# Attention scores: K's low part times Q's high part alone, on halves of the array's rows

## The chip, the core and the metric

The kernel runs on one core of a Trainium2 chip. The metric is device time in microseconds (us) of one execution. TensorE (PE) multiplies matrices in a 128 x 128 array: it loads a stationary operand (LDWEIGHTS), streams the moving operand's columns past it and writes to PSUM. VectorE (DVE), ScalarE (ACT) and GpSimd (POOL) work element by element, SyncE (SP) starts most DMAs. Each engine runs its own instructions in order and waits on semaphores for the others.

## What is computed

Two layers of a hybrid encoder on 1280 tokens (1024 of a prompt, 256 of a sample). The change lies in layer 0's attention. It has 8 heads of a dilated sliding-window mixture (branch a, three patterns) and 8 query heads of grouped-query attention over 2 K/V heads (branch b), all of 64 channels:

```python
s = jnp.einsum('bqhgd,bkhd->bhgqk', qblk, k, preferred_element_type=jnp.float32) * (Dh ** -0.5)
p = jax.nn.softmax(s, axis=-1)
return jnp.einsum('bhgqk,bkhd->bqhgd', p, vf)          # branch b
...
s = jnp.where(valid, s, -jnp.inf)                        # branch a, for each pattern
lse = jax.nn.logsumexp(s, axis=-1); p = jnp.exp(s - lse[..., None])
```

## The kernel before

Everything is f32. For the large products an operand is split in two: hi, which is the value rounded to the matmul's type (fp32r), and lo, the rest. PE then adds up hi·hi, hi·lo and lo·hi (`token_mm`).

Tokens stand in ten tiles of 128 (tiles 0 to 7 the prompt, 8 and 9 the sample). `start` projects x to q, k, v; its step `kvb` (L448) also makes branch b's K. `attention0` then runs 80 items: 4 head pairs of branch b with ten tiles each, then 4 of branch a (units 1 to 4). An item is 128 queries of two heads. For a prompt tile the keys are 8 blocks of 128 in b and 6 in a (these 64 items are called long); for a sample tile 2.

K of a head pair (KH, KL): `k_split` (L334) writes hi and lo of K, each channel twice, to `kd`; `k_trans` (L341) transposes them with 4 PE transposes into PSUM (M in the attention, tr in `start`), and ACT (KH, L349) and DVE (KL, L350) copy them out, scaled. Both halves of the 128 rows hold the same 64 channels. Branch a makes the next unit's K while it works on the present one (`nstep`); branch b makes unit 1's, a tile every fourth item. b's K comes from `start`.

One item i, in the source's order:
- `q_split`: POOL writes Q's hi and lo side by side; `q_trans` (L557): two PE transposes to M, DVE copies them to QS (L563). Rows 0 to 63 of QS are Q's hi, rows 64 to 127 its lo.
- `scores` (L566), a head at a time: QS times KH, then QS times KL, in parts of 512 or 256 columns, on all 128 rows (L587). So all four products of hi and lo are taken. Then DVE's minimum (b: L604; a: with the mask, L598) and ACT's exp (L605, L602). S has two PSUM buffers of 1024 columns.
- `trans` (L608), of item i-1: PE transposes P block by block to T (two PSUM buffers of 512 columns, L615), ACT (L619) and for the last chunk DVE (L617) copies them out.
- `pv` (L627), of item i-2: a transpose of the reciprocal row sums to M (L638, copied by ACT), then V times P on the array's column halves, a head on each (`tile_position`, L645), then DVE's scaling and a DMA.

M and O have one PSUM buffer each. Among the items stand steps of `ada` (modulation vectors for layer 1, matmuls on column strips, L225, every fourth item of b) and of `w_out` (splitting the next weights, ACT and POOL or DVE, every fourth item of a). The source's order isn't the engines' order: a list scheduler in the framework places the instructions by costs and priorities of its own.

Of the kernel before, what the change touches and what calls it, by code (L numbers as in the profile page):

```python
# [18 lines left out]
P = 128  # L19
# [30 lines left out]
class Trunk:  # L50
# [280 lines left out]
        nc.gpsimd.tensor_add(a[:, :n], a[:, :n], b[:, :n])  # L331
        return a

    def k_split(self, kd, k):  # L334

        src = k.rearrange("p (h d) -> p h d", d=HD).unsqueeze(2).to_broadcast([P, 2, 2, HD])
        self.nc.gpsimd.tensor_copy(kd[:, :, 0].bitcast(F32R), src)
        self.nc.gpsimd.tensor_sub(kd[:, :, 1], src, kd[:, :, 0])
        return kd

    def k_trans(self, kd, ps, K, t):  # L341

        nc = self.nc
        ps = ps.rearrange("p (b n) -> p b n", n=P)
# [10 lines left out]
    def start(self):  # L355
# [4 lines left out]
        with ExitStack() as s:  # L360
# [95 lines left out]
            def kvb(t, z):  # L456
                z = z[0]
                r = norm(z[:, :P], 2)
                a = self.rope(z[:, :P], tabs["cosBk"], tabs["sinBk"], 2, 16, t)
                scaled(a, r, 2)  # L460
                kds[t] = self.k_split(t2p.tile([P, 2, 2, 2, HD], F32, name="kd", bufs=3), a[:, :P])
# [36 lines left out]
    def attention0(self):  # L498
        nc, I, tc = self.nc, self.I, self.tc
        self.oT = [self.dram.tile([P, KB, P], F32, name=f"oT{t}") for t in range(NT)]  # L500
        with ExitStack() as s:
# [22 lines left out]
            def k_unit(u):  # L524

                cols = slice(u * P, (u + 1) * P)
                K = self.k_tiles(kp) if u % 2 == 0 else self.k_tiles(self.kbp)

                def load(t):
                    kt = ap.tile([P, P], F32, name="kt", bufs=3)  # L530
                    nc.sync.dma_start(kt, self.zd["ka"][:, t, cols])
                    return kt

                def step(t, kt):
                    self.k_trans(self.k_split(ap.tile([P, 2, 2, 2, HD], F32, name="kd"), kt), self.ps("M"), K, t)
# [13 lines left out]
                it["q"] = q  # L549

            def q_split(it):
                qs = ap.tile([P, 2, 2, HD], F32R, name="qs")
                src = it["q"].rearrange("p (h d) -> p h d", d=HD)
                nc.gpsimd.tensor_copy(qs[:, :, 0], src)
                it["split"] = nc.gpsimd.tensor_sub(qs[:, :, 1], src, self.f(qs[:, :, 0]))
                it["qs"] = qs

            def q_trans(it):
                ps = self.ps("M")
                for h in range(2):  # L560
                    nc.tensor.transpose(ps[:, h * P:(h + 1) * P], self.f(it["qs"][:, h]).rearrange("p a d -> p (a d)"), self.ident)
# [4 lines left out]
            def scores(it, h):  # L566

                br, t = it["br"], it["t"]
                K, kh = it["K"], it["kh"][h]
                blk = lambda X: X[:, kh].rearrange("p (b n) -> p b n", n=P)  # L570
# [8 lines left out]
                S = pb(self.ps("S"))  # L579
                outs, n = [], 0  # L580
                for p in parts:
                    m = len(range(*p.indices(12)))
                    outs.append((S[:, n:n + m], p))
                    n += m
# [3 lines left out]
                pe = ap.tile([P, 8, P], F32, name="pe", bufs=3)  # L588
                st = ap.tile([P, 4], F32, name="st", bufs=8)
                if br == "a":  # L590
                    if t < 8:
                        masks_ = [mask1[:, 3 - cq:7 - cq], pb(mask2[:, hq, cq])]
                    else:
                        masks_ = [pb(masks[:, t - 8])]
                    init, c = NEG, 0
                    for (o, p), mk in zip(outs, masks_):
                        m = o.shape[1]
                        nc.vector.tensor_tensor_reduce(pe[:, c:c + m], o, mk, 1.0, init, op0=OP.add, op1=OP.min,  # L598
                                                       accum_out=st[:, c // 4:c // 4 + 1])
                        init = st[:, c // 4:c // 4 + 1]  # L600
                        c += m
                    it["exp"] = nc.scalar.activation(pe[:, :n], pe[:, :n], AF.Exp, bias=init, scale=-1.0, accum_out=st[:, 2:3])  # L602
                else:
                    nc.vector.tensor_reduce(st[:, 0:1], S[:, :n].rearrange("p b n -> p (b n)"), axis=AX.X, op=OP.min)  # L604
                    nc.scalar.activation(pe[:, :n], S[:, :n], AF.Exp, bias=st[:, 0:1], scale=-1.0, accum_out=st[:, 2:3])  # L605
                it["pe", h], it["sum", h], it["n"] = pe, st[:, 2:3], n

            def trans(it, h):  # L608
                n = it["n"]
# [17 lines left out]
            def pv(it):  # L627
# [12 lines left out]
                nc.scalar.activation(rs, r[:, :P], AF.Copy)  # L640
                o = self.ps("O")
                for b in range(n):
                    for h in range(2):
                        kh = it["kh"][h]
# [20 lines left out]
            for i in range(N + 2):  # L665
# [1139 lines left out]
```

## Time and profile before

| | us |
|---|---|
| median of 3 runs | 3232.96 (3232.84 to 3234.95) |
| the profiled execution | 3234.79 |
| its span, first to last instruction | 3233.0 |
| attention stage, 366.3 to 804.9 | 438.6 |
| branch b, 366.3 to 604.2 | 237.9 |
| branch a, 604.2 to 804.9 | 200.7 |

The mean granted clock was 0.989 of full speed. In the rows below, MATMUL rows are PE's; a timeline row merges successive instructions of one kind and runs from the first's start to the last's modelled end. `128*64` is an instruction on 128 rows and 64 columns of the array, `64*128` one on 64 rows. "Idle" counts only time in which no modelled duration runs. A row of stretches (rows 2) holds: the stretch, its length; the busy time (and count) of PE, PEld, DVE, ACT, POOL; the granted clock, the DMA share, GB/s. A wait (rows 3) holds: us in total, times, longest. A group (rows 4, 7) holds: line, engine, operation, out<-in, shapes, count | busy us, mean ns | idle before it and what ended that.

### The profile page before, as it was taken

The page shows a single profiled execution, that of the slowest core. Times are in us where ns is not written, and L with a number is a line of the kernel's source. Part 1 is how long each engine was busy: PE and PEld are TensorE (multiplying, and loading weights), DVE is VectorE, ACT ScalarE, POOL GpSimd, SP SyncE. Part 2 cuts the span into 40 slices and gives each one's busy share as a digit, 9 for nine tenths or more (in the row PEclk, how much of TensorE's full clock was granted, in tenths as well). Part 3 has the DMA queues.
Part 4 walks back from the last instruction along what each step waited for, and adds up shares of the span by engine and source line. Part 5 has one row for each costly group of instructions (what it writes and reads, how often), then busy time and mean ns, then how long its engine had stood idle before and what let it go on. Part 6 is the DMA issues. An engine that isn't in the chain of part 4 may idle for free. (4 is left out here: it accounts for less than half of the span.)

```text
span 3233.0 us, 49122 instructions
## 1 busy us (share of the span) xinstructions
PE 3125.5 (97%) x18045; PEld 2588.7 (80%) x18045; DVE 1870.6 (58%) x3339; ACT 1435.7 (44%) x2921; POOL 815.3 (25%) x844
## 2 busy tenths in 40 slices
PE   7999999999999999999997998999899999999998
PEld 4777788888788888888886897889677888888886
DVE  4632356677677777544586025137678767644556
ACT  4411366677444444443465225124454444443344
POOL 2421122353014554400000211202214555500000
PEclk9999999999999999999998999999999999999999
DMA  8546622122635666755575313212643666675576
GB/s 268 168 139 212 195 70 74 47 71 57 204 100 176 220 225 214 271 170 177 171 236 171 110 56 101 63 35 66 182 153 113 230 223 219 231 235 172 175 231 207
DMA packets 312790, 520.43 MB, mean 161 GB/s; under 512 B 43093, under 2 KB 172293, under 8 KB 312421
## 3 DMA queue, kind: packets, MB, share of 16 engines
q1 hardware_dynamic: 312405, 516.89, 49.3%
q8 instruction: 142, 2.33, 0.3%
q14 instruction: 99, 0.81, 0.1%
q0 software_dynamic: 144, 0.39, 0.0%
HBM read 359.71 MB, written 157.48 MB: 160 GB/s over the span
## 5 line engine op out<-in xcount | busy, mean ns | idle before, releaser
L1112 PE MATMUL d<-w1l,sh 128*128 128x512 f32 x1120 | 438.2, 391 | 4.6 <-DVE w1l L94 4.6
L1111 PE MATMUL d<-w1h,sh 128*128 128x512 f32 x1120 | 435.9, 391 | 3.6 <-ACT sh L93 2.9
L1113 PE MATMUL d<-w1h,sl 128*128 128x512 f32 x1120 | 437.3, 392 | 1.4 <-DVE ss L99 1.1
L94 DVE TENSOR_TENSOR w1l<-raw,w1h 128x512 fp32r<-128x512 f32 x440 | 356.1, 818 | 115.7 <-ACT w1h L93 112.8
L94 DVE TENSOR_TENSOR sl<-sraw,sh 128x640 fp32r<-128x640 f32 (+2 forms) x256 | 194.7, 762 | 309.6 <-ACT sh L93 309.1
L850 PE MATMUL u<-hTh,w1l 128*128 128x512 f32 (+1 forms) x1056 | 359.2, 340 | 9.4 <-DVE w1l L94 9.4
L850 PE MATMUL u<-hTh,w1h 128*128 128x512 f32 (+1 forms) x1056 | 360.0, 341 | 2.0 <-ACT H L1004 1.7
L850 PE MATMUL u<-hTl,w1h 128*128 128x512 f32 (+1 forms) x1056 | 359.9, 341 | 0.1
L93 ACT ACTIVATE sh<-sraw 128x640 fp32r<-128x640 f32 (+2 forms) x256 | 172.7, 675 | 393.3 <-PE d L1112 367.2
L93 ACT ACTIVATE w1h<-raw 128x512 fp32r<-128x512 f32 x444 | 275.2, 624 | 141.1 <-PE u L850 112.1
L283 PE MATMUL z<-wh,hTh 128*128 128x512 f32 (+2 forms) x800 | 275.3, 362 | 2.9 <-ACT wh L93 1.7
L285 PE MATMUL z<-wh,hTl 128*128 128x512 f32 (+2 forms) x800 | 269.9, 354 | 1.7 <-DVE hTl L165 1.7
L283 PE MATMUL z<-wl,hTh 128*128 128x512 f32 (+2 forms) x800 | 270.0, 354 | 1.1 <-DVE wl L94 0.5
L1112 PEld LDWEIGHTS d<-w1l,sh 128*128 128x128 f32 x1120 | 210.7, 188 | 51.2 <-DVE w1l L94 8.0
L1111 PEld LDWEIGHTS d<-w1h,sh 128*128 128x128 f32 x1120 | 210.9, 188 | 50.5 <-ACT sh L93 5.5
L1113 PEld LDWEIGHTS d<-w1h,sl 128*128 128x128 f32 x1120 | 210.7, 188 | 48.2 <-DVE sl L94 5.4
L850 PEld LDWEIGHTS u<-hTh,w1l 128*128 128x128 f32 x1056 | 202.8, 192 | 31.4 <-DVE w1l L94 9.8
L850 PEld LDWEIGHTS u<-hTh,w1h 128*128 128x128 f32 x1056 | 202.9, 192 | 24.7 <-ACT H L1004 1.9
L850 PEld LDWEIGHTS u<-hTl,w1h 128*128 128x128 f32 x1056 | 203.0, 192 | 22.3 <-DVE hTl L165 1.1
L283 PEld LDWEIGHTS z<-wh,hTh 128*128 128x128 f32 x800 | 146.0, 189 | 37.4 <-issue 9.1
L285 PEld LDWEIGHTS z<-wh,hTl 128*128 128x128 f32 x800 | 146.2, 189 | 26.4 <-DVE hTl L165 3.5
L283 PEld LDWEIGHTS z<-wl,hTh 128*128 128x128 f32 x800 | 146.5, 189 | 19.6 <-DVE wl L94 1.9
(371 smaller groups left out, 6412.3 us busy)
## 6 DMA issues: line engine op xcount, KB each, us to landing
raw<-in_w_ff SPq DMA_DIRECT2D x128, 512.0 KB, 4.2
sraw<-hd SPq DMA_DIRECT2D x192, 320.0 KB, 3.0
wada<-in_w_ada SPq DMA_DIRECT2D x44, 1024.0 KB, 5.4
hd<-H SPq DMA_DIRECT2D x64, 640.0 KB, 4.0
wd<-raw SPq DMA_DIRECT2D x64, 512.0 KB, 3.0
raw<-in_w_ff SPq DMA_DIRECT2D x128, 256.0 KB, 3.7
raw<-wd SPq DMA_DIRECT2D x128, 256.0 KB, 3.2
hd<-part SPq DMA_DIRECT2D x96, 320.0 KB, 3.4
```

The source lines that it names most:

```text
L93: self.nc.scalar.activation(hi, src, AF.Copy)
L94: (eng or self.nc.vector).tensor_sub(lo, src, self.f(hi))
L283: nc.tensor.matmul(o, hi[:, k, sl], w[k][i][:, c], start=first and i == 0, stop=False)
L285: nc.tensor.matmul(o, lo[:, k, sl], w[k][0][:, c], start=False, stop=last)
L850: self.nc.tensor.matmul(o, a[:, k], b, start=(start and k == 0 and i == 0), stop=(stop and k == 3 and i == 2))
L1111: nc.tensor.matmul(ps, o[0][:, sl], w[0], start=first, stop=False)
L1112: nc.tensor.matmul(ps, o[0][:, sl], w[1], start=False, stop=False)
L1113: nc.tensor.matmul(ps, o[1][:, sl], w[0], start=False, stop=last)
```

## The change

- K is copied twice by POOL (`k_twice`), transposed (2 transposes for 4), and split behind it: ACT copies KH out of PSUM, DVE forms KL from the same PSUM and KH.
- Q's second head has lo in rows 0 to 63 and hi in rows 64 to 127.
- Scores of both heads are issued together. KH takes all 128 rows as before. KL takes Q's hi alone, on 64 rows: head 0 on the lower half, head 1 on the upper. lo·lo is no longer taken.
- The exps (`expo`) stand behind both heads' scores, each after the transposes of item i-1 of its head. The reciprocal's transpose goes to spare columns of O, not M. The K step stands behind `pv`, except a unit's last. `pe` has 4 buffers (3).

```diff
-    def k_split(self, kd, k):
-        src = k.rearrange("p (h d) -> p h d", d=HD).unsqueeze(2).to_broadcast([P, 2, 2, HD])
-        self.nc.gpsimd.tensor_copy(kd[:, :, 0].bitcast(F32R), src)
-        self.nc.gpsimd.tensor_sub(kd[:, :, 1], src, kd[:, :, 0])
+    def k_twice(self, kd, k):
+        self.nc.gpsimd.tensor_copy(kd, k.rearrange("p (h d) -> p h d", d=HD).unsqueeze(2).to_broadcast([P, 2, 2, HD]))
...
         for h in range(2):
-            for i in range(2):
-                nc.tensor.transpose(ps[:, 2 * i + h], kd[:, h, i].rearrange("p a d -> p (a d)"), self.ident)
+            nc.tensor.transpose(ps[:, h], kd[:, h].rearrange("p a d -> p (a d)"), self.ident)
         sl = slice(t * P, (t + 1) * P)
-        nc.scalar.activation(K[0][:, :, sl], ps[:, 0:2], AF.Copy, scale=-0.125)
-        nc.vector.tensor_scalar(K[1][:, :, sl], ps[:, 2:4], -0.125, None, op0=OP.mult)
+        nc.scalar.activation(K[0][:, :, sl], ps, AF.Copy, scale=-0.125)
+        nc.vector.scalar_tensor_tensor(K[1][:, :, sl], ps, -0.125, self.f(K[0][:, :, sl]), op0=OP.mult, op1=OP.subtract)
...
-                nc.gpsimd.tensor_copy(qs[:, :, 0], src)
-                it["split"] = nc.gpsimd.tensor_sub(qs[:, :, 1], src, self.f(qs[:, :, 0]))
+                nc.gpsimd.tensor_copy(qs[:, 0:4:3], src)
+                it["split"] = nc.gpsimd.tensor_sub(qs[:, 1:3], src, self.f(qs[:, 0:4:3]))
...
-                for i in range(2):
-                    for o, p in outs:
-                        nc.tensor.matmul(o, it["QS"][:, h], blk(K[i])[:, p], start=(i == 0), stop=(i == 1))
+                    for o, p in zip(outs[h], parts):
+                        nc.tensor.matmul(o, it["QS"][:, h], blk(0, h)[:, p], start=True, stop=False)
+                for j, p in enumerate(parts):
+                    for h in range(2):
+                        r = slice(64 * h, 64 * h + 64)
+                        nc.tensor.matmul(outs[h][j], it["QS"][r, h], blk(1, h)[r, p], start=False, stop=True)
...
-                r = self.ps("M")
-                nc.tensor.transpose(r[:, :P], it["rb"].rearrange("p h d -> p (h d)"), self.ident)
+                o = self.ps("O")
+                nc.tensor.transpose(o[:, P:2 * P], it["rb"].rearrange("p h d -> p (h d)"), self.ident)
...
-                    scores(it, 0)
-                if 0 <= i - 1 < N:
-                    trans(items[i - 1], 0)
+                    scores(it)
                 if i + 1 < N:
                     q_trans(items[i + 1])
-                if it:
-                    scores(it, 1)
-                if 0 <= i - 1 < N:
-                    trans(items[i - 1], 1)
-                if todo is not None:
+                for h in range(2):
+                    if 0 <= i - 1 < N:
+                        trans(items[i - 1], h)
+                    if it:
+                        expo(it, h)
+                if todo == NT - 1:
                     nstep(todo, nk[todo])
                 if 0 <= i - 2 < N:
                     pv(items[i - 2])
+                if todo is not None and todo < NT - 1:
+                    nstep(todo, nk[todo])
```

What the scheduler makes of it, at three places. First PE in branch b, one long item before (S scores, T transposes of P, M<-qs the next Q's transposes, O<-pT the value products):

```order
L587 MATMUL S<-KH,QS 128x512 x2
L587 MATMUL S<-KL,QS 128x512 x2
L615 MATMUL T<-ident,pe 128x128 x8
L561 MATMUL M<-ident,qs 128x128 x2
L587 MATMUL S<-KH,QS 128x512 x2
L587 MATMUL S<-KL,QS 128x512 x2
L615 MATMUL T<-ident,pe 128x128 x8
L638 MATMUL M<-ident,rb_3580 128x128
L645 MATMUL O<-pT,vt 64x128 x16
```

and one of after (L586 is KH, L590 KL, L622 T, L651 the value products, L645 the reciprocal's transpose):

```order
L586 MATMUL S<-KH,QS 128x512 x2
L590 MATMUL S<-KL,QS 128x512 x2
L586 MATMUL S<-KH,QS 128x512
L651 MATMUL O<-pT,vt 64x128 x16
L586 MATMUL S<-KH,QS 128x512
L590 MATMUL S<-KL,QS 128x512 x2
L559 MATMUL M<-ident,qs 128x128 x2
L622 MATMUL T<-ident,pe 128x128 x6
L645 MATMUL O<-ident,rb_3633 128x128
L622 MATMUL T<-ident,pe 128x128 x8
```

Here the first head's two KL stand ahead of the second head's KH, and the value products in the middle of that; the transposes of P are no longer split by scores.

Second PE in branch a, from the second head's KH of one long item on, after (with buffer numbers: S_8315 is head 0, S_8318 head 1):

```order
L586 MATMUL S_8318<-KH_7323,QS_8259 128x512
L586 MATMUL S_8318<-KH_7323,QS_8259 128x256
L590 MATMUL S_8315<-KL_7324,QS_8259 128x512
L590 MATMUL S_8318<-KL_7324,QS_8259 128x512
L590 MATMUL S_8315<-KL_7324,QS_8259 128x256
L590 MATMUL S_8318<-KL_7324,QS_8259 128x256
L622 MATMUL T_8339<-ident_114,pe_8248 128x128 x4
L622 MATMUL T_8345<-ident_114,pe_8248 128x128 x2
L645 MATMUL O_8367<-ident_114,rb2_8287 128x128
L559 MATMUL M_8333<-ident_114,qs_8310 128x128 x2
L622 MATMUL T_8351<-ident_114,pe_8252 128x128 x4
L622 MATMUL T_8357<-ident_114,pe_8252 128x128 x2
```

and a long item of a before:

```order
L587 MATMUL S<-KL,QS 128x256
L615 MATMUL T<-ident,pe 128x128 x6
L561 MATMUL M<-ident,qs 128x128 x2
L587 MATMUL S<-KH,QS 128x512
L587 MATMUL S<-KH,QS 128x256
L587 MATMUL S<-KL,QS 128x512
L587 MATMUL S<-KL,QS 128x256
L615 MATMUL T<-ident,pe 128x128 x6
L347 MATMUL M<-ident,kd 128x128 x4
L645 MATMUL O<-pT,vt 64x128 x9
```

In a the heads alternate in KL, and T's third chunk follows the first two after one to three small transposes, where scores stood between.

Third DVE in branch b, reductions of an item's two heads, the cast of the next QS and the copy of a T chunk, before:

```order
L604 TENSOR_REDUCE st_5138<-S_5132 128x1
L236 TENSOR_TENSOR shc_131<-shc_131,bcol_127 128x16
L563 CAST QS_5157<-M_5154 128x256
L604 TENSOR_REDUCE st_5165<-S_5159 128x1
L617 COPY pT_5168<-T_5175 128x512
```

and after, where KL was paired:

```order
L605 TENSOR_REDUCE st_3504<-S_3493 128x1
L605 TENSOR_REDUCE st_3507<-S_3496 128x1
L561 CAST QS_3512<-M_3509 128x256
L624 COPY pT_3528<-T_3535 128x512
L630 RECIPROCAL rc_3630<-st_3504 128x1
```

The cast, which stood between the two reductions, stands behind both.

## Rows read from the trace of the kernel before

**Rows 1.** Engines on the page: busy us, share of the span, instructions.

```profile
PE 3125.5 (97%) x18045; PEld 2588.7 (80%) x18045; DVE 1870.6 (58%) x3339; ACT 1435.7 (44%) x2921; POOL 815.3 (25%) x844
```

**Rows 2.** Busy time by engine in branch b and branch a of the attention stage.

```profile
366.30:604.20 237.90, 235.47 (x2219) 192.15 (x2219) 144.91 (x301) 150.24 (x321) 56.53 (x151) 1.00 0.29 88
604.20:804.90 200.70, 199.88 (x1820) 168.01 (x1820) 142.72 (x526) 146.97 (x349) 92.74 (x204) 1.00 0.21 61
```

**Rows 3.** PE's waits, 366 to 805 us: engine, line, releaser; first, fourth, last of six.

```profile
PE M L638 <- DVE KL L350: 1.7, 7, 0.3
...
PE T L615 <- ACT pT L619: 0.3, 1, 0.3
...
PE S L587 <- ACT pe L605: 0.2, 1, 0.2
```

**Rows 4.** Groups of instructions by shape on PE, 366 to 805 us.

```profile
L615 PE MATMUL T<-ident,pe 128*128 128x128 f32 x960 | 134.4, 273 | 0.4 <-ACT pT L619 0.3
L587 PE MATMUL S<-KH,QS 128*128 128x512 f32 x192 | 78.0, 459 | 0.7 <-DVE QS L563 0.5 <-ACT pe L605 0.2
L587 PE MATMUL S<-KL,QS 128*128 128x512 f32 x192 | 66.7, 398 | 0.0
```

**Rows 5.** Timeline of PE in branch b: start, duration of the merged row, count.

```profile
484.99 1.52 PE L645 MATMUL O<-pT,vt 128*64 128x128 f32 x22
...
490.10 0.65 PE L645 MATMUL O<-pT,vt 128*64 128x128 f32 x6
490.68 0.74 PE L587 MATMUL S<-KH,QS 128*128 128x512 f32 x2
491.26 0.63 PE L587 MATMUL S<-KL,QS 128*128 128x512 f32 x2
491.73 0.49 PE L615 MATMUL T<-ident,pe 128*128 128x128 f32 x3
...
541.64 0.28 PE L587 MATMUL S<-KL,QS 128*128 128x256 f32 x1
541.76 0.38 PE L615 MATMUL T<-ident,pe 128*128 128x128 f32 x2
...
547.65 0.38 PE L615 MATMUL T<-ident,pe 128*128 128x128 f32 x2
547.96 0.43 PE L645 MATMUL O<-pT,vt 128*64 128x128 f32 x2
```

**Rows 6.** Timeline of PE at two bursts of the mLSTM's scores.

```profile
2148.00 0.66 PE L1531 MATMUL m<-ident,kT 128*128 128x128 f32 x4 [0.61 <-ACT kT L1374]
2148.58 1.49 PE L1604 MATMUL S<-qT,kT 64*128 64x128 f32 x14
...
2163.52 1.16 PE L1604 MATMUL S<-qT,kT 64*128 64x128 f32 x8 [0.16 <-DVE DT L1606]
2164.61 0.55 PE L1531 MATMUL m<-ident,kT 128*128 128x128 f32 x3
```

**Rows 7.** Groups by shape on ACT and DVE, 366 to 805 us.

```profile
L619 ACT ACTIVATE pT<-T 128x512 f32<-128x512 f32 x160 | 92.1, 596 | 65.6 <-PE T L615 65.6
L605 ACT ACTIVATE pe<-S,st 128x1024 f32<-128x1024 f32 x64 | 71.5, 1117 | 7.0 <-DVE st L604 6.1
...
L604 DVE TENSOR_REDUCE st<-S 128x1 f32<-128x1024 f32 x64 | 78.4, 1224 | 32.4 <-PE S L587 32.0
L563 DVE CAST QS<-M 128x256 fp32r<-128x256 f32 x79 | 33.2, 420 | 8.2 <-PE M L561 7.8
```

**Rows 8.** Timeline of DVE: first reduction of two items, four items apart.

```profile
504.12 1.22 DVE L604 TENSOR_REDUCE st<-S 128x1 f32<-128x1024 f32 x1
...
530.71 1.23 DVE L604 TENSOR_REDUCE st<-S 128x1 f32<-128x1024 f32 x1
```

**Rows 9.** Timeline of PE: first scores of two successive items of branch a.

```profile
682.70 0.61 PE L587 MATMUL S<-KH,QS 128*128 128x512 f32 x2
...
688.35 0.62 PE L587 MATMUL S<-KH,QS 128*128 128x512 f32 x2
```

More of the change, by code (lines that the diff above doesn't have):

```diff
@@ L460, in kvb @@
                 scaled(a, r, 2)
-                kds[t] = self.k_split(t2p.tile([P, 2, 2, 2, HD], F32, name="kd", bufs=3), a[:, :P])
+                kds[t] = self.k_twice(t2p.tile([P, 2, 2, HD], F32, name="kd", bufs=3), a[:, :P])
                 for u in ([t - 2] if t > 1 else []) + ([t - 1, t] if t == NT - 1 else []):
@@ L534, in step @@
                 def step(t, kt):
-                    self.k_trans(self.k_split(ap.tile([P, 2, 2, 2, HD], F32, name="kd"), kt), self.ps("M"), K, t)
+                    self.k_trans(self.k_twice(ap.tile([P, 2, 2, HD], F32, name="kd"), kt), self.ps("M"), K, t)
                     if t in (3, 7):
@@ L551, in q_split @@
             def q_split(it):
-                qs = ap.tile([P, 2, 2, HD], F32R, name="qs")
+                qs = ap.tile([P, 4, HD], F32R, name="qs")
                 src = it["q"].rearrange("p (h d) -> p h d", d=HD)
-                nc.gpsimd.tensor_copy(qs[:, :, 0], src)
-                it["split"] = nc.gpsimd.tensor_sub(qs[:, :, 1], src, self.f(qs[:, :, 0]))
+                nc.gpsimd.tensor_copy(qs[:, 0:4:3], src)
+                it["split"] = nc.gpsimd.tensor_sub(qs[:, 1:3], src, self.f(qs[:, 0:4:3]))
                 it["qs"] = qs
@@ L560, in q_trans @@
                 for h in range(2):
-                    nc.tensor.transpose(ps[:, h * P:(h + 1) * P], self.f(it["qs"][:, h]).rearrange("p a d -> p (a d)"), self.ident)
+                    nc.tensor.transpose(ps[:, h * P:(h + 1) * P], self.f(it["qs"][:, 2 * h:2 * h + 2]).rearrange("p a d -> p (a d)"), self.ident)
                 QS = ap.tile([P, 2, P], F32R, name="QS")
@@ L564, in q_trans, with scores @@
                 it["QS"] = QS
[L566 to L570, printed above, removed]
+            def scores(it):
+                br, t, K = it["br"], it["t"], it["K"]
+                blk = lambda i, h: pb(K[i][:, it["kh"][h]])
                 if t >= 8:
@@ L578, in scores @@
                     parts = [slice(4 * hq, 4 * hq + 4), slice(a, b + 1, b - a)]
[L579 to L584, printed above, removed]
-                for i in range(2):
-                    for o, p in outs:
-                        nc.tensor.matmul(o, it["QS"][:, h], blk(K[i])[:, p], start=(i == 0), stop=(i == 1))
@@ L588, in scores @@
[L588 to L592, printed above, removed]
-                    else:
[L594 to L605, printed above, removed]
@@ L606, in scores @@
-                it["pe", h], it["sum", h], it["n"] = pe, st[:, 2:3], n
+                outs, S = [[], []], []
+                for h in range(2):
+                    x, n = pb(self.ps("S")), 0
+                    for p in parts:
+                        m = len(range(*p.indices(12)))
+                        outs[h].append(x[:, n:n + m])
+                        n += m
+                    S.append(x[:, :n].rearrange("p b n -> p (b n)"))
+                    for o, p in zip(outs[h], parts):
+                        nc.tensor.matmul(o, it["QS"][:, h], blk(0, h)[:, p], start=True, stop=False)
@@ new lines, in scores @@
+                for j, p in enumerate(parts):
+                    for h in range(2):
+                        r = slice(64 * h, 64 * h + 64)
+                        nc.tensor.matmul(outs[h][j], it["QS"][r, h], blk(1, h)[r, p], start=False, stop=True)
+                for h in range(2):
+                    pe = ap.tile([P, 8, P], F32, name="pe", bufs=4)
+                    st = ap.tile([P, 4], F32, name="st", bufs=8)
+                    if br == "a":
+                        masks_ = [mask1[:, 3 - cq:7 - cq], pb(mask2[:, hq, cq])] if t < 8 else [pb(masks[:, t - 8])]
+                        init, c = NEG, 0
+                        for o, mk in zip(outs[h], masks_):
+                            m = o.shape[1]
+                            nc.vector.tensor_tensor_reduce(pe[:, c:c + m], o, mk, 1.0, init, op0=OP.add, op1=OP.min,
+                                                           accum_out=st[:, c // 4:c // 4 + 1])
+                            init = st[:, c // 4:c // 4 + 1]
+                            c += m
+                    else:
+                        init = st[:, 0:1]
+                        nc.vector.tensor_reduce(init, S[h], axis=AX.X, op=OP.min)
+                    it["pe", h], it["sum", h], it["max", h] = pe, st[:, 2:3], init
+                    it["S", h] = pe[:, :n].rearrange("p b n -> p (b n)") if br == "a" else S[h]
@@ L608, in trans, with expo @@
+                it["n"] = n
+            def expo(it, h):
+                pe = it["pe", h][:, :it["n"]].rearrange("p b n -> p (b n)")
+                it["exp"] = nc.scalar.activation(pe, it["S", h], AF.Exp, bias=it["max", h], scale=-1.0, accum_out=it["sum", h])
             def trans(it, h):
@@ L636, in pv @@
                     vb = [4 * hq + c for c in range(4)] + [4 * (1 - hq) + cq, NT + 1 - hq]
[L637 to L638 removed]
+                o = self.ps("O")
+                nc.tensor.transpose(o[:, P:2 * P], it["rb"].rearrange("p h d -> p (h d)"), self.ident)
                 rs = ap.tile([P, P], F32, name="rs", bufs=2)
[L640 to L641 removed]
+                nc.scalar.activation(rs, o[:, P:2 * P], AF.Copy)
                 for b in range(n):
@@ L698, in attention0 @@
                             next(self.w_out, None)
-                    scores(it, 0)
-                if 0 <= i - 1 < N:
-                    trans(items[i - 1], 0)
+                    scores(it)
                 if i + 1 < N:
                     q_trans(items[i + 1])
-                if it:
-                    scores(it, 1)
-                if 0 <= i - 1 < N:
-                    trans(items[i - 1], 1)
-                if todo is not None:
+                for h in range(2):
+                    if 0 <= i - 1 < N:
[3 more added lines that the diff above has]
+                if todo == NT - 1:
                     nstep(todo, nk[todo])
```

2 lines of the change are left out of this document (1 added, 1 removed).

## The prediction

> **What bounds the kernel now.** I read the page first: TensorE (PE) is busy for 97% of the span [rows 1]. A busy PE is not yet a PE at its limit, so I cut the trace by stage and looked at PE's waits. The change works in the attention stage, 366.3 to 804.9 us, and for 2 us in the projection before it. The stage falls into branch b (40 items, 237.9 us) and branch a (40 items, 200.7 us), both at the full granted clock; ACT is busy for 63% and 73% of them, DVE for 61% and 71% [rows 2]. In all of the stage PE waits for another engine for 3.5 us, over six kinds of wait, 1.7 of them in one [rows 3]. So here PE is limited by issue: an item costs what its instructions take one after another, and what PE is saved or charged moves the end, until something else waits.
>
> Prices of one instruction, from start to start, as merged rows give them: n instructions of a kind last (n-1) intervals and one modelled duration, which is 0.27 us for 128 columns, 0.39 for 512 and 0.28 for 256 [rows 4, 5]. A transpose takes (0.49-0.27)/2 = 0.11. A 512-column score matmul takes 0.63-0.39 = 0.23 to 0.24 (I use 0.231), one of 256 columns 541.76-541.64 = 0.12 (I use 0.118). The value product ("PV", L645) runs as two passes a matmul, on two halves of the array's columns: 22 passes in 1.52 us are 0.06 each, so a pass of one head and one of the other share one interval of 0.11.
>
> Changing between the whole array and a part of it costs extra. Into PV: the last transpose before it holds PE until 547.96, 0.20 us after its own start (547.65+0.38-0.27) where 0.11 is usual, and PV's first two passes take 0.43 and not 0.38: 0.09+0.05. Out of PV: again 0.20 in place of 0.11, then two KH matmuls last 0.74 where two KL last 0.63: 0.09+0.11 [rows 5]. That shows in the means too: KH, which mostly comes after PV or a transpose, 459 ns, KL behind it 398 [rows 4].
>
> The change's new form, 64 rows of the array, stands in this trace once, in the mLSTM's scores [rows 6]. Eight of them last 1.16 us: 7 intervals in 0.89, 0.11 more than 7 at 0.112. The transpose before the first burst holds PE 0.19 to 0.20 us, and the one after the second starts 0.20 after the last matmul; three of those last 0.55 and not 0.49. So a visit to 64 rows costs 0.09+0.11 on the way in and 0.09+0.06 on the way out: 0.35 (0.40 where a KH follows). The 14 matmuls of the first burst take 13 intervals in 1.22 us, 0.094 each: some of them, on different halves, ran together. That the halves overlap is thus shown, but not for 512 columns.
>
> **The change part by part, on PE.** The order tells what the source doesn't: the scheduler doesn't keep the four KL matmuls of an item together. I counted the rows of the stage on PE, in both orders.
> - KL: before 192 of 512 and 96 of 256 columns, 55.7 us. After, 59 pairs of 512 and 40 of 256 have the two heads side by side; 74 and 16 stand alone or behind their own head. That is 133 x 0.231 + 56 x 0.118 = 37.3: -18.4. Branch a has 71 of the 99 pairs, b only 28.
> - Visits to 64 rows: 111 runs (70 in b, 41 in a), 0.34 to 0.40 each: +38.
> - K's transposes: 80 fewer x 0.109 = -8.7.
> - PV stands in 81 runs, not 131, and 2 of them are of odd length, not 88. 50 visits fewer at 0.31 are -15.6, and 14 of those left adjoin a 64-row run that has their change already, -3; each odd run leaves half of the array empty for two passes, 86 x 0.109 = -9.4.
> - Ada's products (column strips too) stand in more pieces: +2.4.
> Together -14.7, and by branch, with each branch's own counts: b 234.0 before and 239.6 after, +5.6; a 193.7 and 173.8, -19.9. The 428 counted of before stand against 438.6 measured; I carry the rest over unchanged.
>
> **Projection.** 20 transposes fewer, in a stretch that PE also fills: -2.2.
>
> **New waits.** (1) Transposed blocks of P go through two PSUM buffers (T), emptied in half of the cases by ACT, 0.60 a copy [rows 7]. Before, KH and KL of one head (0.9 us) stood between the first two chunks and the next two. After, the chunks of both heads follow each other with only one small transpose or three between. The third chunk may start at 0.33 (four starts) + 0.27 + 0.60 = 1.20 us after the first; in b PE is there after 8 transposes and one more, at 0.98, in a after 6 and one to three more, at 0.76 to 0.98. So PE waits 0.22 to 0.44; queued behind that transpose are PV and the next item's scores, so all of PE. Below, the wait can be nothing (a copy that is there in time, as now: 0.3 us in all [rows 3]); above, an exp of 1.12 us ahead of the copy adds all of itself [rows 7]. I take 0.33 for the 64 long items: +10.6 in each branch.
> (2) In b a paired item ends both heads' scores together, and DVE's order has both reductions ahead of the cast of the next QS: 0.39 + 1.22 + 1.22 + 0.42 = 3.25 us from the last pair's start to the cast's end [rows 5, 7]. PE has in that time 0.23 + 0.15 + 18 transposes 1.96 + one more 0.11 + the wait of (1) = 2.8, and then needs QS, or the buffer M that the cast empties. Some 0.4 late in about 13 items: +5. It is between 0 and 12 (0.9 late if the wait of (1) is none and a K transpose stands first).
> (3) DVE's KL now reads ACT's KH, so a K tile may hold M for a copy longer: at worst 40 times the 0.42 of a cast of that size [rows 7], at best nothing; PE's wait for M behind KL is 1.7 us in all now [rows 3], and I take 0. POOL loses a subtraction for each K tile, and PE doesn't wait for POOL: 0.
> Two long items show the sizes: four items of b, with an ada step and a K tile among them, now take 530.71-504.12 = 26.6 us [rows 8]. An unpaired item of after is, by the rows of the order, 4 KH 0.92 + 4 KL 0.92 + 18 transposes 1.96 + one 0.11 + PV 1.74 + two visits 0.75 + PV's 0.34 = 6.75, where the one of before has 6.0. In a an item takes 688.35-682.70 = 5.65 [rows 9]; after, KH 0.70 + KL 0.35 + one visit 0.35 + 17 transposes 1.85 + PV 1.31 + its visit 0.29 = 4.85, and 5.2 with the wait.
>
> **The sum:** b +5.6 + 10.6 + 5 = +21.2; a -19.9 + 10.6 = -9.3; projection -2.2. In all +9.7 us, on the profiled execution's 3234.8 (span 3233.0), which lies 1.8 above the median of 3233.0. Forecast: 3243.
>
> The Trainium skill, "TensorEngine Tiling (Array Packing)", Theoretical Speedup, grants two 64-row tiles up to twice the speed; where KL is paired the trace's prices agree on the matmuls alone, 0.46 in place of 0.92, and the visit takes 0.35 of it back. By that rule alone the sum would be 38 lower, 3205. The same page, PSUM Bottleneck, says that a faster TensorE leaves the copies out of PSUM as they were and that these may become the limit; [rows 3] show no such wait now, and by that rule wait (1) is the term to watch.
>
> **Rivals.**
> - Waits stay away: the scheduler filled the gaps, as it does now with its 3.5 us. Then issue alone counts: -14.7 - 2.2 = -16.9, 3216. For it: PE's few waits in [rows 3], with the same buffers. Against: 18 transposes in a row had 0.9 us of scores between them.
> - A visit to 64 rows is nearly free for this kind of matmul: 38 less, 3205. For it only that [rows 6] are of another input type; the same 0.09 stands on each change of shape in [rows 5].
> - No measurable change: half of the waits of (1) and (2), 13 less, is 3230; visits at 0.29 in place of 0.34 are 6 less, 3237.
> - Slower by more: the halves don't overlap for 512 columns. The 99 pairs then cost 59 x 0.231 + 40 x 0.118 = 18.3 more, 3261. It decides as soon as fewer than half of the pairs overlap. For it: no row has such a pair. Against: the overlaps in [rows 6].
> - Exps ahead of the copies lengthen wait (1) past 0.5 us: 3253 and up.
>
> **How the numbers follow.** Two measurements of this kernel can be told apart by about 0.2%, 6.5 us. Chances: the forecast (3240 to 3252) 0.42, longer waits 0.08, no overlap 0.11: slower 0.61. No change 0.17. Waits away 0.17 and free visits 0.05: faster 0.22. The range of 0.8 reaches from 3218 (nearly all waits away) to 3260 (nearly no overlap); the forecast's own is 3239 to 3252.
>
> **What would show it.** Right: branch b's stretch longer by some 20 us and a's shorter by some 10; KL pairs that start within 0.01 us in a, and 0.23 apart in most of b; some 20 us of PE waits for ACT's pT and DVE's QS; transposes that start 0.20 after a KL. Wrong: b as long as before, or a KL followed by its next instruction at the price of a KH.

## The result, and the profile after

| | before | after |
|---|---|---|
| median, us | 3233.1 (3232.84 to 3234.95, 4 runs) | 3284.24 (3276.61 to 3286.87, 4 runs) |
| ratio, 95% interval | | 1.0153 (1.0135 to 1.0171) |
| profiled execution, span | 3234.79, 3233.0 | 3286.03, 3284.3 |
| start of the first `ot` (an item's scaled output) | 380.5 | 398.8 |
| end of branch b's last reduction | 603.3 | 641.5 |
| end of branch a's last masked reduction | 800.9 | 842.7 |
| start of the next stage (y) | 804.5 | 851.3 |

The change made the kernel slower by 1.5%, some 51 us, where the forecast was 9.7 us slower, and outside the range given (3218 to 3260). By place, the extra time is +18.3 us by the first `ot`, +19.9 in the rest of b, +3.6 in a, +5.0 between a's last reduction and y, and +4.5 behind. Of the 4.5 some 2.5 may be the clock: it is 0.50 from 850 to 856 in after, behind waits of PE, and 1.00 at the same place of before, and y starts at 851.3 (an estimate, half of the 5 us up to 856). The 4.5 isn't clear of chance: the part behind y's start takes 2423 to 2433 us in the profiled executions of all the kernels here.

The page's engines line of after, which answers to [rows 1], shows PE busy for longer, but for a smaller share of a longer span:

```profile
PE 3135.3 (95%) x17945; PEld 2548.7 (78%) x17945; DVE 1870.2 (57%) x3339; ACT 1427.9 (43%) x2921; POOL 777.5 (24%) x794
```

Stretches of after, the columns as in [rows 2]: the start of the attention in two pieces, then b from its first S on, then a:

```profile
366.00:374.30 8.30, 0.70 (x3) 0.31 (x3) 0.42 (x1) 0.00 (x0) 1.81 (x6) 0.50 1.02 355
374.30:400.00 25.70, 23.30 (x124) 14.56 (x125) 12.27 (x23) 12.10 (x23) 4.56 (x13) 0.72 0.48 145
374.30:642.20 267.90, 258.00 (x2187) 179.45 (x2188) 146.34 (x300) 147.73 (x320) 47.31 (x138) 0.97 0.21 63
642.20:851.70 209.50, 188.53 (x1772) 143.85 (x1771) 142.33 (x528) 143.82 (x351) 71.54 (x176) 1.00 0.21 61
```

Three things stand in them. From 366.00 to 374.30, where PE worked on the first scores before, it is busy for 0.70 us, at a granted clock of 0.50 (the lower level, 1.2 GHz), while the DMA engines are full. In the next 26 us the clock averages 0.72. And branch a has 21 us without PE busy, where [rows 2] has 0.8.

PE's waits in the attention stage of after, which answer to [rows 3] with its 3.5 us:

```profile
PE T L622 <- ACT pT L626: 15.1, 41, 1.2
PE M L559 <- POOL qs L553: 11.1, 1, 11.1
PE O L651 <- ACT rs L647: 2.9, 7, 0.4
PE M L344 <- DVE QS L561: 2.3, 3, 1.0
PE M L344 <- DVE rc L630: 2.3, 1, 2.3
PE S L586 <- DVE QS L561: 1.7, 3, 0.7
```

Here pT is the copy of T, rs ACT's copy of rb's transpose (rb holds the reciprocal row sums, rc DVE's result ahead of it), qs Q split by POOL and kd a tile of K.

The timeline of PE at the stage's first scores, and of one tile of a with K's, Q's and P's transposes around it:

```profile
373.08 0.69 PE L559 MATMUL M<-ident,qs 128*128 128x128 f32 x2 [11.13 <-POOL qs L553]
374.29 2.08 PE L586 MATMUL S<-KH,QS 128*128 128x512 f32 x4 [0.52 <-DVE QS L561]
...
700.00 0.94 PE L586 MATMUL S<-KH,QS 128*128 128x512 f32 x4
700.87 0.62 PE L590 MATMUL S<-KL,QS 64*128 64x512 f32 x4
701.42 0.55 PE L622 MATMUL T<-ident,pe 128*128 128x128 f32 x3
701.80 0.41 PE L559 MATMUL M<-ident,qs 128*128 128x128 f32 x2
702.05 0.49 PE L622 MATMUL T<-ident,pe 128*128 128x128 f32 x3
702.38 0.27 PE L645 MATMUL O<-ident,rb 128*128 128x128 f32 x1
703.07 0.88 PE L622 MATMUL T<-ident,pe 128*128 128x128 f32 x6 [0.42 <-ACT pT L626]
```

The first row shows an idle time of 11.13 us that POOL's qs ends, and two transposes of q at the lower clock: 0.69 us, where two take 0.41 at 701.80. In the second piece the four KL (the two heads paired) hold PE from 700.87 to 701.42, and between the transpose of rb at 702.38 and the next block of T at 703.07 lie 0.69 us in place of 0.11, 0.42 of it idle: T's wait of the prediction.

### The profile page after: what moved, and what is told of

Its sections match the earlier page's. It is cut to its first block, busy times and chain, and to the rows that moved or that the text cites. A ratio compares the mean times of both kernels' runs of the same rounds, so it can differ in the third digit from the quotient of the medians.

```text
span 3284.3 us, 48890 instructions
## 1 busy us (share of the span) xinstructions
PE 3135.3 (95%) x17945; PEld 2548.7 (78%) x17945; DVE 1870.2 (57%) x3339; ACT 1427.9 (43%) x2921; POOL 777.5 (24%) x794
## 5 line engine op out<-in xcount | busy, mean ns | idle before, releaser
L857 PEld LDWEIGHTS u<-hTl,w1h 128*128 128x128 f32 x1056 | 203.1, 192 | 22.3 <-DVE hTl L165 1.0
L626 ACT ACTIVATE pT<-T 128x512 f32<-128x512 f32 (+1 forms) x208 | 107.2, 545 | 129.4 <-PE T L622 111.6
```

Source lines behind the costliest of these rows:

```text
L626: nc.scalar.activation(pT[:, b0:b0 + m], ps[:, :m], AF.Copy)
L857: self.nc.tensor.matmul(o, a[:, k], b, start=(start and k == 0 and i == 0), stop=(stop and k == 3 and i == 2))
```

## Experiments

Eleven kernels, each timed beside the kernel before. Four of them, and the change itself as the last row, take it apart in steps, in this one order. Us are the ratio times 3234.4, the median of before in one of the series; a step's is uncertain by 3 to 8.

| kernel | median | ratio (95%) | against the row above, us |
|---|---|---|---|
| K transposed first, alone | 3226.65 | 0.9972 (0.9962 to 0.9981) | -9.1 (to before) |
| and rb's transpose in O | 3217.82 | 0.9939 (0.9919 to 0.9959) | -10.7 |
| and both heads' scores together, exps apart, K step behind PV | 3245.39 | 1.0035 (1.0023 to 1.0047) | +31.0 |
| and KL on 64 rows | 3269.03 | 1.0104 (1.0089 to 1.0119) | +22.3 |
| and pe's fourth buffer: the change | 3284.24 | 1.0153 (1.0135 to 1.0171) | +15.8 |

The third step also holds Q's new order of hi and lo. Of its 31.0 the two profiled executions show 20.6 (spans 3220.7 and 3241.3).

Two more numbers serve below. PE's time from each start to the next, put down to the kind of the first, from the first `ot` to a's last masked reduction, us (a wait is in the kind that stands before it):

| kernel | scores | T | q | rb | PV | K's transposes | ada | all |
|---|---|---|---|---|---|---|---|---|
| before | 123.9 | 103.5 | 11.6 | 15.4 | 131.7 | 21.6 | 12.2 | 420 |
| K alone | 125.3 | 103.9 | 12.3 | 14.4 | 130.6 | 13.0 | 12.2 | 412 |
| and rb in O | 130.3 | 106.4 | 15.6 | 9.1 | 113.8 | 11.4 | 17.7 | 405 |
| and heads together | 125.0 | 112.0 | 19.1 | 25.6 | 116.9 | 11.3 | 15.8 | 426 |
| and 64 rows | 138.7 | 113.7 | 21.1 | 24.6 | 117.0 | 11.9 | 16.2 | 443 |
| after | 131.2 | 112.2 | 22.6 | 37.3 | 115.9 | 7.7 | 16.1 | 443 |

A run is a group of successive matmuls of one kind. PV stands in 131 runs before, 132 with K alone, 85 with rb in O and 81 in the three below it. KL on 64 rows stands in 124 runs with 84 pairs (two heads' matmuls that start together) with three buffers of pe, and in 111 with 99 pairs in the change.

**The start: pe's fourth buffer.** Two kernels without it, or with it alone.

```diff
-                pe = ap.tile([P, 8, P], F32, name="pe", bufs=4)
+                pe = ap.tile([P, 8, P], F32, name="pe", bufs=3)
```

> The changed kernel with three buffers of pe (bufs=3) in place of four, nothing else. With it the order of SyncE's queue at the start of the attention is that of the kernel before (q, then kt, then masks, then V). Theory (the fourth buffer of pe, 4 KB of a partition, moves the q tiles to memory that frees later, and this alone delays the start): the first S matmul is back near 363 to 367, and branch b ends 18 to 21 us earlier, at 620 to 623. What three buffers cost in branch a isn't known: the reduction of head 1 then has to wait until the tile before's head 0 is transposed, 0 to 0.5 us in each of 40 items, so the whole is 3262 to 3285. Rival (the order of scores itself delays the start): the first S stays at 374 and the time is 3277 or more.

Measured: 3269.03 (3266.91 to 3271.88), 1.0104 (1.0089 to 1.0119), 15.8 less; the first S at 363.1, as the first theory has it. But b's last reduction, at 631.3, is 10.2 earlier than with four buffers and not 18 to 21: from the first `ot` (385.6) on, b takes 245.7 in place of 242.7. So by the traces 13.2 of the 15.8 stand ahead of the first `ot`; the buffer changes the order of the matmuls behind it too.

The opposite: `k_twice` and `k_trans` of the change put into the kernel before, then once more with `bufs=4` for `pe`.

> The kernel before with one part of the change alone: K transposed first and then split (two transposes in place of four for each tile, DVE's scalar_tensor_tensor from ps and KH for the lo part); scores, q and the order of the loop are those of before. By the prediction's terms: projection -2.2, K transposes in the attention -8.7, so 3222 (3219 to 3226). Rival (a DVE instruction that waits for ACT's KH and then reads it adds a wait in each of the 50 tiles, as K's transposes shared M with q's): 0.1 to 0.3 us each, so no gain or 3233 to 3240.

> As the run with K transposed first alone, but with four buffers of pe, of which this loop needs only three: nothing in the computation differs, only the addresses, and with them SyncE's order, where the first q loads fall behind V's and the masks' loads. Theory (late start): 15 to 21 us over the run with three buffers, with PE waiting some 11 us ahead of the first S and a granted clock near 0.5 to 0.75 in the 25 us behind it. Rival (the start doesn't count): the same time as with three buffers, within 2 us.

Measured: 3226.65 (3222.84 to 3229.56) and 3238.11 (3235.11 to 3242.0), 0.9972 (0.9962 to 0.9981) and 1.0013 (1.0003 to 1.0022): K's part gains 9.1 of the 10.9 forecast, just outside of what was expected, and a buffer that this loop doesn't need costs 13.3, a little less than expected; PE waits 11.0 us ahead of the first S there. SyncE's timeline shows where it comes from. Without the buffer:

```profile
355.42 0.92 SPq L545 DMA_DIRECT2D q<-zqb  x2
...
364.26 0.85 SPq L507 DMA_DIRECT2D mask<-in_mask  x2
365.16 0.42 SPq L507 DMA_DIRECT2D masks<-in_mask_s  x1
365.63 0.43 SPq L513 DMA_DIRECT2D vt<-zvb  x1
```

and with it:

```profile
361.50 0.42 SPq L513 DMA_DIRECT2D vt<-zvb  x1
362.03 4.71 SPq L507 DMA_DIRECT2D mask<-in_mask  x2
366.78 0.43 SPq L507 DMA_DIRECT2D masks<-in_mask_s  x1
367.26 1.38 SPq L545 DMA_DIRECT2D q<-zqb  x3
```

The q loads (L545) start at 355.42 without it, and with it at 367.26, behind V and the masks, whose two issues take 4.71. Since nothing uses the buffer, it can act only through the addresses of the tiles and the order that the scheduler then chooses; that q's tiles come to lie on memory that is freed later is argued, not shown. PE's stretches of the two kernels, the first without the buffer, the others with it:

```profile
364.00:400.00 36.00, 34.74 (x298) 27.87 (x299) 22.99 (x42) 23.75 (x47) 8.07 (x24) 1.00 0.74 232
```

```profile
366.00:374.60 8.60, 0.69 (x2) 0.29 (x2) 0.42 (x1) 0.00 (x0) 1.77 (x6) 0.50 1.06 370
374.60:400.00 25.40, 24.29 (x190) 19.62 (x191) 15.97 (x29) 15.68 (x31) 5.71 (x17) 0.93 0.53 155
```

PE loses the idle time and then works at 0.93 of the clock for 25 us, less of a loss than the 0.5 to 0.75 expected; in the changed kernel it was 0.72. The Trainium skill, "TensorE: Matmul & The Clock Gate", What's actually happening, names 1.2 GHz as TensorE's clock when idle: the 0.50 above agrees.

Putting the q loads ahead by hand, with four buffers:

```diff
-            for n, m in (("mask1", mask1), ("mask2", mask2), ("mask_s", masks)):
-                nc.sync.dma_start(m, I[n])
...
-            Ks = {0: (*self.KB, v_tile("b", slice(0, P)))}
+            with self.after(items[0]["ql"], items[1]["ql"]):
+                Ks = {0: (*self.KB, v_tile("b", slice(0, P)))}
+                for n, m in (("mask1", mask1), ("mask2", mask2), ("mask_s", masks)):
+                    nc.sync.dma_start(m, I[n])
```

> The changed kernel, with the first two q loads of the attention put ahead of the masks' and V's loads in SyncE's queue, nothing else. Theory (the late start): some 18 to 21 us of the 51 come from SyncE's order, which in the changed kernel puts the first q loads at 366.9, behind V's load and the masks (4.86 us in issue), where they stood at 357.7 before. Then the first S matmul starts near 365 to 368 in place of 374.3, the granted clock of 374 to 400 is 1.00 in place of 0.72, the first write of ot ends near 382 in place of 398.8, and the whole takes 3262 to 3270 (ratio to the changed kernel 0.994 to 0.995). Rival (the start is absorbed, since the attention is held later by ACT and DVE in any case): the first S comes earlier but branch b still ends at 641 and the time stays at 3277 to 3287.

Measured: 3278.88 (3277.69 to 3280.15), 1.0134 (1.0119 to 1.0149): 6 less than the change by the ratios, which their intervals don't tell from nothing, and in the rival's range. By the trace the first S is at 371.5, not 365 to 368, and b's last reduction at 639.0, 2.5 earlier. The loads start at 361.42 only, behind two loads of ada's weights, and POOL gets its q at 369.45, when V's and the masks' loads (from 363.67 on) are on their way too. So this place in the queue gives back little; what else holds the q loads up isn't shown.

**The 64 rows.**

```diff
-                        nc.tensor.matmul(outs[h][j], it["QS"][r, h], blk(1, h)[r, p], start=False, stop=True)
+                        nc.tensor.matmul(outs[h][j], it["QS"][:, h], blk(1, h)[:, p], start=False, stop=True)
```

> The changed kernel with three buffers of pe, and with KL's matmuls over all 128 rows again (QS whole against KL whole, so lo times lo is added too); both heads' scores still stand together. Compared with the run with three buffers alone (3269). Theory (matmuls on 64 rows cost more than their overlap saves): PE's time in scores in branch b falls from 78.6 to about 66, that in T and q falls by some 8 more as no 64-row matmul stands ahead of them, so b is 20 to 27 us shorter, and a 0 to 8 shorter: 3235 to 3250. Rival (the common order of both heads and its waits for T's buffers is the cost, not the rows): scores grow by the lost overlap, some 18 us over both branches, and the time is 3270 to 3288.

Measured: 3245.39 (3243.08 to 3247.89), 1.0035 (1.0023 to 1.0047): the 64 rows cost 22.3, against +20 forecast from visits and pairs for the change's order (by the same prices some +26 for the 124 runs and 84 pairs of this one), and the theory of the rows holds. By the traces b is 13 shorter (not 20 to 27), a 4.6, and the first `ot` comes 3.9 earlier; scores fall by 13.7, T and q together by 3.7, not 8.

> The kernel before with K transposed first (3226.7), and KL's matmuls on 64 rows with the new order of q's hi and lo, but each head's scores for themselves as before: no matmul of the other head stands beside it. Theory (each run of 64-row matmuls costs PE 0.2 to 0.4 us, and only a neighbour on the other half gives time back): 160 runs by 0.2 to 0.4, +32 to +64 us, so 3259 to 3291, and PE's time in scores in b up from 65.7 to 82 to 95. Rival (the runs of 64 rows are free, the loss lies in the order of both heads): 3224 to 3230.

The edit, on the kernel with K first and the change's order of q:

```diff
-                for i in range(2):
-                    for o, p in outs:
-                        nc.tensor.matmul(o, it["QS"][:, h], blk(K[i])[:, p], start=(i == 0), stop=(i == 1))
+                r = slice(64 * h, 64 * h + 64)
+                for o, p in outs:
+                    nc.tensor.matmul(o, it["QS"][:, h], blk(K[0])[:, p], start=True, stop=False)
+                for o, p in outs:
+                    nc.tensor.matmul(o, it["QS"][r, h], blk(K[1])[r, p], start=False, stop=True)
```

Measured: 3282.27 (3278.48 to 3285.23), 1.0144 (1.0129 to 1.0159), 55.6 over K alone, and 87 us of scores in b, both within the first theory. The trace has 167 runs of 64 rows and no overlap: 0.33 each, where the prediction used 0.34 to 0.40. Where it comes from shows in the same place of two timelines, with 64 rows

```profile
442.45 0.73 PE L585 MATMUL S<-KH,QS 128*128 128x512 f32 x2
443.11 0.73 PE L587 MATMUL S<-KL,QS 64*128 64x512 f32 x2
443.77 1.09 PE L615 MATMUL T<-ident,pe 128*128 128x128 f32 x8
444.70 0.38 PE L559 MATMUL M<-ident,qs 128*128 128x128 f32 x2
```

and with 128:

```profile
441.88 0.72 PE L584 MATMUL S<-KH,QS 128*128 128x512 f32 x2
442.44 0.64 PE L584 MATMUL S<-KL,QS 128*128 128x512 f32 x2
442.91 1.04 PE L612 MATMUL T<-ident,pe 128*128 128x128 f32 x8
443.78 0.27 PE L635 MATMUL M<-ident,rb 128*128 128x128 f32 x1
```

KH's two are followed after 0.66 in place of 0.56, KL's two after 0.66 in place of 0.47, and the eight transposes last 0.05 to 0.06 longer: 0.34. In the median, a KL of 512 columns on 64 rows holds PE for 0.338 where another of the same rows follows, and 0.232 on 128 rows. The 22.3 were measured on 124 such runs; 124 x 0.33 = 41, less the 22.3, leaves about 19 (uncertain by 7) that the overlaps of 84 pairs give back, where the prediction's prices give 16. In after the 111 runs and 99 pairs that the prediction counted are all in the trace, a pair's second matmul 4 ns behind the first.

**T's buffers and the order of both heads.** Four kernels tried to take PE's waits away, all with three buffers of pe.

> The changed kernel with three buffers of pe, and with PV of the item two back put between the transposes of head 0 and head 1 in place of behind both. Compared with 3269. Theory (T's two buffers make PE wait behind the transpose of rb, 10.6 us of PE's time from the start of rb's transposes to the next in a, 14.0 in b, against 6.5 and 7.9 where the scores stood between): 5 to 12 us are saved, 3257 to 3264. Rival (ACT's copies are late by as much at any other place, since ACT's queue has the exps between them): the wait moves to another instruction, 3266 to 3272.

> Both of the last: three buffers of pe, KL's matmuls over 128 rows, both heads' scores together, PV between the two heads' transposes. Theory (rows and T's buffers both cost, and their costs add): 5 to 12 us below the run with 128 rows alone, 3225 to 3242, near the kernel before with K transposed first (3226.7), and with fewer runs of PV. Rival (without the 64-row matmuls PE reaches T's buffers sooner and waits as long as it saved): within 3 us of the run with 128 rows alone.

```diff
                     if it:
                         expo(it, h)
+                    if h == 0 and 0 <= i - 2 < N:
+                        pv(items[i - 2])
...
-                if 0 <= i - 2 < N:
-                    pv(items[i - 2])
```

Measured: 3258.25 (3257.12 to 3262.86), 1.0075 (1.0058 to 1.0092), against 3269.03 with 64 rows: 9 less, the size that the first theory had. With 128 rows 3252.05 (3249.22 to 3254.91), 1.0051 (1.0036 to 1.0066), against 3245.39: 5 more by the ratios, which their intervals don't tell from none, so the first theory fails there. PE then waits 5.3 us for ACT's rs, where it waited 3.4. Nor is the theory's reason right with 64 rows: the waits at T are no shorter (3.6 and 3.1 us, before 2.4 and 3.0). What the trace shows is another order, KL in 95 runs with 123 pairs in place of 124 with 84: 29 runs at 0.33 and 39 pairs more can make up the 9 us alone, and on 128 rows they count for nothing.

> The changed kernel with three buffers of pe and KL over 128 rows (3245.4), with both heads' exps put ahead of the copies of T in the order of the source, in place of one exp behind each head's copies. Theory (ACT's place of the exps makes little of the cost where the scheduler may still move them): 3242 to 3250. Rival, the prediction's own (exps of 1.12 us ahead of the copies lengthen the wait for T's two buffers): PE's time behind the transposes of rb and T grows by 0.5 to 1 us in each long item, 3265 to 3290. Other rival (the exps come too late now, and S's two buffers hold the next scores): 3230 to 3240.

```diff
-                for h in range(2):
-                    if 0 <= i - 1 < N:
-                        trans(items[i - 1], h)
-                    if it:
-                        expo(it, h)
+                for h in range(2):
+                    if it:
+                        expo(it, h)
+                for h in range(2):
+                    if 0 <= i - 1 < N:
+                        trans(items[i - 1], h)
```

> The changed kernel with three buffers of pe and KL over 128 rows (3245.4), with the copy of the second T tile on DVE for both heads in place of head 1 alone, so that ACT and DVE empty T's two buffers side by side. Theory (PE waits for T's buffers as ACT copies three tiles of four one after the other at 0.6 us: 11 us of rb's growth over the kernel before with K first, and part of T's 8): 8 to 15 us less, 3230 to 3238. Rival (DVE is then late with its reductions, 0.6 us in each item more on DVE): 3243 to 3260. Other rival (the extra is not T's buffers, but the weight loads seen at each change of kind of matmul): 3243 to 3247.

```diff
-                    if h == 1 and b0 + m == n:
+                    if b0 + m == n:
                         nc.vector.tensor_copy(pT[:, b0:b0 + m], ps[:, :m])
```

Measured: 3259.14 (3256.86 to 3263.57), 1.0073 (1.0055 to 1.0091), and 3266.47 (3259.75 to 3267.47), 1.009 (1.0071 to 1.0108): 12 and 18 more than without, by the ratios. The exps ahead lengthen b alone (by 10.9; a stays at 194 us); that is less than the 20 to 45 of the prediction's rival. Sharing the copies makes T's own wait shorter and DVE late, which was the rival's case, and it splits PV into 107 runs for 81, which take 10.1 us more. PE's longest waits with the exps first

```profile
PE S L586 <- DVE QS L561: 8.9, 15, 0.8
PE T L622 <- ACT pT L626: 5.8, 24, 0.5
PE O L651 <- ACT rs L647: 3.8, 9, 0.5
```

and with the copies shared:

```profile
PE S L586 <- DVE QS L561: 11.1, 17, 1.4
PE O L651 <- ACT rs L647: 4.6, 11, 0.4
PE T L622 <- ACT pT L626: 3.0, 8, 0.9
```

and in the kernel they start from:

```profile
PE T L622 <- ACT pT L626: 4.3, 13, 0.9
PE O L651 <- ACT rs L647: 3.4, 8, 0.4
...
PE S L586 <- DVE QS L561: 2.1, 3, 0.8
```

What is shown: with both heads' scores together, work of ACT or DVE that is added or put ahead in an item comes back as a wait of PE, for QS above all, though each is busy for 58 to 71% of the stage in the kernel they start from. Which order of the two would take the 31 us away stays open.

**The part that gains.** The transpose of rb into O's spare half, on top of K alone:

```diff
-                r = self.ps("M")
-                nc.tensor.transpose(r[:, :P], it["rb"].rearrange("p h d -> p (h d)"), self.ident)
+                o = self.ps("O")
+                nc.tensor.transpose(o[:, P:2 * P], it["rb"].rearrange("p h d -> p (h d)"), self.ident)
                 rs = ap.tile([P, P], F32, name="rs", bufs=2)
-                nc.scalar.activation(rs, r[:, :P], AF.Copy)
-                o = self.ps("O")
+                nc.scalar.activation(rs, o[:, P:2 * P], AF.Copy)
```

> The kernel before with K transposed first (3226.7), and from the change one thing more: rb is transposed into the unused half of O's bank in place of M, and rs copied from there. Theory (it takes one user from M, where q's and K's transposes and rb's wait for each other; PE's waits on M in that run are under 2 us in all): 3222 to 3228. Rival (the transpose of rb now has to wait until ot of the item before is read out of O, and this is part of the 18.7 us that the common order cost): 3230 to 3245.

Measured: 3217.82 (3212.99 to 3222.46), 0.9939 (0.9919 to 0.9959), 0.6% faster than before, below the expected 3222, and the best version found. The theory's reason can't be the main one, since PE's waits on M in the run with K alone are 0.8 us; what falls is PV's time, by 16.8 us, as its runs go from 132 to 85 by this edit alone.

## Why the prediction was wrong

By the steps, forecast and measured in us, the measured ones from the table of steps:

| step | forecast | measured |
|---|---|---|
| K's transposes, attention and projection | -10.9 | -9.1 |
| PV's runs -28.0, ada +2.4 | -25.6 | -10.7 (rb in O) |
| waits (1) and (2) | +26.2 | +31.0 (heads together) |
| visits +38, pairs -18.4 | +19.6 | +22.3 |
| late start of the attention | not there | +15.8 (fourth buffer) |
| sum | +9.3 (+9.7 by branches) | +49.3 |

The steps don't hold the terms of their row alone: "heads together" is all that the common order changes, waits or not.

- **The step that failed first is one that isn't in the sum.** The prediction costed `pe`'s fourth buffer at nothing, without naming it: it looked at three places of the order and not at SyncE's queue at the head of the stage, where the first q loads go from 357.68 to 366.89, behind the masks. +15.8, shown by taking the buffer away and by adding it alone (13.3).
- **The second is PV's -28.** Its counts came true: 131 runs became 81, and of 88 with an odd number of matmuls 2 are left. PV's own time falls by 15.8, half inside the runs and half at their ends. The rest of a visit's price lies in the kinds beside it, and there it wasn't saved: with rb in O alone PV falls by 16.8, rb and K's transposes by 6.9, but scores (+5.0), ada (+5.5, not 2.4), q (+3.3) and T (+2.5) grow by 16.3. Two reasons are in the trace. Ada stands in 31 runs for 22, and 5.5 for nine more is 0.6 each, where the prediction took 0.27. And 25 of PV's runs now stand behind a score matmul, where 2 did; that one then holds PE some 0.09 longer, some 2 us in all. For the rest the runs show no reason.
- **Waits (1) and (2)** came near in sum, by luck. rb's time, which holds wait (1), grows by 21.9 from before to after (forecast 21.2), but by 4.9 in b and 17.0 in a, where 10.6 was taken for each, and much of a's comes with the fourth buffer: with three, rb takes 24.6 in all and not 37.3. Wait (2) failed: in b, where it was forecast at 5, PE waits for QS for 0.2 us behind the first item; of the 4.0 us of "DVE QS" (1.7 and 2.3) 3.5 stand in a and 0.5 ahead of the first S. (That ACT empties T in half of the cases is a slip: it is three chunks of four.) Of the common order's step 16.5 stand behind rb's transposes. T and q take 8.1 and 6.8 more than with K alone: behind PV, ada, a K step or a wait the first transpose often holds PE for 0.165 and not 0.109. In part it is a shift between kinds, as a transpose of q counts 0.03 ahead of a KH, whose own time then holds the rest, and 0.109 ahead of T.
- **Branches.** b was forecast at +21.2 and grew by 19.9 from the first `ot` on, also by luck, with more issue (scores alone +12.6, where all issue was to be +5.6) and less wait. a was forecast at -9.3 and grew by 3.6: its scores gained 5.3, PV 7.7 and K's transposes 10.7, and rb lost 17.0, q 6.2 and T 3.6.
- **The 64 rows** were right, count (111 runs, 99 pairs), price (0.33 against 0.34 to 0.40) and sum, and so the rivals "free visits" and "no overlap" are out. The make-up was not: a pair of 512 columns holds PE for 0.33, where it was taken at 0.231 beside the visit, and two on 128 rows for 0.46, so a pair is 1.4 times as fast, not twice. The last, exps ahead of the copies, is half right: it lengthens b by 10.9 where it is forced, but in the changed kernel ACT's copies are late (15.1 us) without it.
- **Behind a**, y starts 8.6 after the last reduction, 3.6 before: with rb in O alone it is 6.9. The last items' transpose of rb, its copy and PV now share one bank, with nothing beside them: PE waits 0.57, 0.43, 0.54 and 0.37 us for ot and rs there, where it waited 0.19. Not forecast.

## What to carry to other kernels

Take a change's steps one by one before believing its sum: here two gained 20 us together (K first, rb in O) and three lost 69. A buffer more is not free where a scheduler sets addresses and order: compare the DMA queue at the start of the stage, not only the engines in its middle. And on halves of the array's rows, weigh each run (0.33 us) against what its overlaps give back (here some 19 us over 124 runs, 0.15 each).

## What the runs showed of the hardware

- Two 512-column f32 matmuls that follow each other on the same 64 rows start 0.338 us apart, on 128 rows 0.232, though the weight load (PEld) takes 183 ns in the one and 188 in the other. What differs by as much is the load's start: on 64 rows it comes 0.107 behind the start of the matmul before it, in all 115 successions of the run with each head for itself, on 128 rows 0.002 to 0.005, in 110 of 115 with K alone. On opposite halves the second matmul starts 4 ns after the first, and the next pair 0.334 after that. The Trainium skill, "TensorE: Matmul & The Clock Gate", The mechanism, says that a weight load overlaps with running matmuls only on other row groups, and beside that names a background weight buffer. On 128 rows the trace shows the load beside a running matmul of the same rows, which only the second allows; on 64 it starts later, but still within the 0.232 that 512 columns take on 128 rows.
- After some 11 us of idle PE the granted clock was 0.50, and over the next 25 us 0.72 in the change and 0.93 with K alone and four buffers (PE busy for 23.30 and 24.29 us there).
